# Copies of k issued by GpSimd, and each bias fetched behind the put of the squares, in the attention of a hybrid decoder block

## The chip, the cores and the metric

The kernel runs on one core of one Trainium2 chip. Times are device microseconds for one execution. The engines are TensorE (PE; its weight loads are PEld), VectorE (DVE), ScalarE (ACT), GpSimd (POOL) and SyncE (SP). SP does no arithmetic here: it issues most of the DMAs, strictly in order.

## The reference, cut to what matters

One layer of a decoder block on 512 tokens of width 1024: a retention branch and a forgetting-attention branch, merged by gates, then a feed-forward part. The change lies in the forgetting attention, which has 8 heads of width 64:

```python
c = jnp.cumsum(log_f, axis=1).transpose(0, 2, 1)
...
s = jnp.einsum('bhqd,bhkd->bhqk', q_blk, kh).astype(jnp.float32) * scale
s = s + c_blk[..., None] - c[:, :, None, :]
s = jnp.where(mask[None, None], s, -jnp.inf)
p = jax.nn.softmax(s, axis=-1)
return jnp.einsum('bhqk,bhkd->bhqd', p.astype(vh.dtype), vh)
```

All is float32. Queries come in 4 blocks of 128, and a block needs the keys up to its own end only.

## The kernel before, in words

**Products in three parts.** PE takes each float32 operand as a sum of a rounded high part and the rest, and forms high x high, low x high and high x low. Splitting a weight tile takes a cast on ACT (`wh<-raw`, L164) and a subtraction on DVE (`wl<-raw,wh`, L165). Two raw buffers and three pairs of split buffers go round. For the scores the split of q fills both halves of the partitions (high in one, low in the other), so one matmul does two of the three products if the high part of k stands in both halves as well. That is the copy of k: `fox_prep` casts k into one half of `tk` on ACT (L775) and a DMA copies this half into the other (L777). The low part of k goes into `kl`, whose other half GpSimd has set to zero (L991).

**The chain of a head.** The heads go in pairs `a` with `e` = 0, 1; here they are called heads 0 to 7. `chain` lists 32 steps, each head's query blocks from the last (512 keys) down to the first (128 keys). A step is: GpSimd adds the causal mask to 128 columns of the bias `cb` (L798); PE forms the scores into a bank `sc` or `tp`; DVE adds the bias, negates and finds the extremum (L804, tiles `pr` and `nm`); ACT takes the exponential (L806). Two steps later DVE transposes the weights in 32 x 32 squares into `psq` (L818). When a head's squares are all there, `fox_put` writes them to DRAM (`pd<-psq`) and `fox_get` reads them back with rows and columns exchanged in four DMAs (`pT<-pd`). For an odd head the reciprocal row sums go the same way (`rd<-rt`, `rw<-rd`, two DMAs). Then `fox_values` multiplies by v for a pair on PE, DVE scales (L857), ACT casts `ofh` and DVE subtracts `ofl` (L866).

**The bias.** `fox_bias(h)` reads one row of 512 numbers from DRAM (`cd`) into all 128 partitions of a `cb` buffer. There are three such buffers, so a bias waits for the one three heads before to be used up.

**What sets the order.** The instructions of PE are chained by hand (`in_order`), and between the steps of the attention `Fill` puts in matmuls of the gate projections, by a running account of time. SP's DMAs of this stage are chained in the order of the program (`move`, L71). The order on DVE, ACT and GpSimd, and the place of a bias among SP's DMAs, come from a scheduler that goes by the order of the program and by its own estimates.

**Completion counters.** DMAs of SP and ACT are counted on eight counters, DMAHW0 to DMAHW7, given out in turn. A DMA whose counter is still in use by an older one waits for that.

Of the kernel before, what the change touches and what calls it, by code (L numbers as in the profile page):

```python
# [23 lines left out]
FH, FD = 8, 64  # L24
# [27 lines left out]
def block_kernel(ctx: ExitStack, tc, x, xT, c_early, c_tab, c_late, w_vf, w_tok, w_vg, w_qk, w_a, w_y, w_o, w_gu, w_gl, w_dn, w_dh, out):  # L52
    nc = tc.nc
# [15 lines left out]
    def move(to, src):  # L69

        ins = nc.sync.dma_start(out=to, in_=src)  # L71
        if moves[0]:
            if moves[1] is not None:
                after(ins, moves[1])
            moves[1] = ins
        return ins
# [9 lines left out]
    def f32(ap):  # L86
        return ap.bitcast(F32)
# [72 lines left out]
    def split_raw(raw, width=1024):  # L160
        pool, bufs = next_pool(part_pools, 1)
        h = pool.tile([P, WP if pool is wp else 1024], F32R, name="wh", tag="wh", bufs=bufs)
        l = pool.tile([P, WP if pool is wp else 1024], F32R, name="wl", tag="wl", bufs=bufs)
        split_raw.last = (nc.scalar.copy(out=h[:, :width], in_=raw[:, :width]),  # L164
                          tt(out=l[:, :width], in0=raw[:, :width], in1=f32(h)[:, :width], op=ALU.subtract))  # L165
        return h, l
# [55 lines left out]
    for k in range(NK):  # L222
        h, l = first_units[k // 2]
# [274 lines left out]
    gp = nc.gpsimd  # L498
    ret = [{} for _ in range(NT)]
    fox = {}  # L500
# [215 lines left out]
    def fox_bias(h):  # L716

        cb = fwk.tile([P, S], F32, name="cb", tag="cb", bufs=CBUF)
        move(cb, cd[h:h + 1, :].broadcast_to([P, S]))
        return cb  # L720
# [42 lines left out]

    turn_next.n = 0

    def fox_prep(a, e, part):

        r, o = ((ra, rb), (rb, ra))[e]
        zr = (kf, qf)[part].rearrange("p c (u j) -> p u c j", j=32)[r, 4 * a:4 * a + 4]
        h = fwk.tile([P, S], F32R, name=("tk", "tq")[part], tag=f"{('tk', 'tq')[part]}{e}", bufs=2)  # L770

        def parted(f):
            return f.rearrange("p (u c j) -> p u c j", c=4, j=32)

        nc.scalar.copy(out=parted(h[r]), in_=zr)  # L775
        if part == 0:
            nc.scalar.dma_start(out=f32(h)[o], in_=f32(h)[r])  # L777
        to = h[o] if part else kls[a % 2][e][r]
        tt(out=parted(to), in0=zr, in1=parted(f32(h)[r]), op=ALU.subtract)
        fox[("k", "q")[part], a, e] = h  # L780
# [6 lines left out]
    def fox_scores(a, e, i):  # L787

        tq, tk, kl = fox["q", a, e], fox["k", a, e], kls[a % 2][e]
        if i == NT - 1:  # L790
            fox["cb"] = fox["bias"].pop(0)
            if e == 0:
                fox["rs", a] = sm.tile([P, 2, NT], F32, name="rs", tag="rs", bufs=2)
        cb = fox["cb"]
        n = (i + 1) * P
        m = max(n, 256)
        qs = slice(i * P, n)
        gp.tensor_tensor(out=cb[:, qs], in0=cb[:, qs], in1=mask, op=ALU.add)  # L798
        sc = next_bank()
        mm(sc[:, :m], lhsT=tq[:, qs], rhs=tk[:, :m], start=True, stop=False)  # L800
        mm(sc[:, :m], lhsT=tq[:, qs], rhs=kl[:, :m], start=False, stop=True)
        pr = fwk.tile([P, n], F32, name="pr", tag=f"pr{i}", bufs=1)
        nm = sm.tile([P, 1], F32, name="nm", tag="nm", bufs=4)
        fox_scores.last = nc.vector.tensor_tensor_reduce(out=pr[:, :n], in0=cb[:, :n], in1=sc[:, :n], scale=-1.0, scalar=3e38,  # L804
                                       op0=ALU.add, op1=ALU.min, accum_out=nm)
        fox["last"] = act(out=pr[:, :n], in_=pr[:, :n], func=AF.Exp, scale=-1.0, bias=nm, accum_out=fox["rs", a][:, e, i:i + 1])  # L806
        fox["pr", a, e, i] = pr

    def fox_turn(a, e, i):

        if i == NT - 1:
            fox["sq", a, e] = fwk.tile([P, 4, 10, 32], F32, name="psq", tag="psq", bufs=PSQ)
        pr, to = fox["pr", a, e, i], fox["sq", a, e].rearrange("p b c j -> p c b j")
        squares_ = pr.rearrange("p (k b j) -> p k b j", b=4, j=32)
        for k0, k1, step in ((0, min(i, 1), 3), (2, i, 1)):
            if k1 >= k0:
                c = TRI[k0] + i
                nc.vector.transpose(out=to[:, c:c + (k1 - k0) * step + 1:step], in_=squares_[:, k0:k1 + 1])  # L818

    def fox_put(a, e):  # L820

        pd = fox["pd", e] = drp.tile([4, 32, 4, 320], F32, name="pd", tag=f"pd{e}")
        move(pd.rearrange("g m b x -> (g m) (b x)"), fox["sq", a, e].rearrange("p b c j -> p (b c j)"))
        if e:
            nc.vector.reciprocal(out=ri[:, 0:2 * NT], in_=fox["rs", a].rearrange("p e i -> p (e i)"))
            rt = sm.tile([P, 32], F32, name="rt", tag="rt", bufs=1)
            nc.vector.transpose(out=rt, in_=ri)
            fox["rt"] = rt

    def put_scale():  # L830

        rd = fox["rd"] = drp.tile([P, 32], F32, name="rd", tag="rd")
        move(rd, fox["rt"])

    def fox_get(a, e):

        pT = fox["pT", a, e] = fwk.tile([P, 4, 320], F32, name="pT", tag="pT", bufs=PT)
        for b in range(4):
            move(pT[32 * b:32 * b + 32], fox["pd", e][:, :, b, :].rearrange("g m x -> m g x"))
        if e:  # L840
            rw = fox["rw", a] = fwk.tile([P, S], F32, name="rw", tag="rw", bufs=1)
            for h, rows in enumerate((ra, rb)):
                row = fox["rd"].rearrange("(g x) j -> x g j", g=4)[4 * h:4 * h + 4].rearrange("i g j -> g i j")
                row = bass.AP(tensor=row.tensor, offset=row.offset, ap=[[0, FD], [32 * 32, 4], [1, 4 * 32]])
                move(rw[rows].rearrange("p (g x) -> p g x", g=4), row)

    def fox_values(a):

        av = next_bank()
        o = av.rearrange("p (g i j) -> p g i j", g=4, i=NT)  # L850
        for k in range(NT):
            c = TRI[k] + k
            for e in range(2):
                mm(o[e * FD:(e + 1) * FD, :, k:, :].rearrange("p g i j -> p g (i j)"), lhsT=vf[:, k, (2 * a + e) * FD:(2 * a + e + 1) * FD],
                   rhs=fox["pT", a, e][:, :, 32 * c:32 * (c + NT - k)], start=k == 0, stop=k == NT - 1)
        o = o.rearrange("p g i j -> p i g j")
        first = tt(out=o, in0=o, in1=fox["rw", a].rearrange("p (g i j) -> p i g j", i=NT, g=4), op=ALU.mult)  # L857
        after(first, split_raw.last[1])
        if a == 3:
            after(first, y_ret.last)  # L860
        h, l = (f[:, a, :].rearrange("p (i g j) -> p i g j", i=NT, g=4) for f in (ofh, ofl))
        cast = nc.scalar.copy(out=h, in_=o)
        after(cast, split_raw.last[0])
        if a == 3:
            after(cast, sigmoid.last)
        tt(out=l, in0=o, in1=f32(h), op=ALU.subtract)  # L866
# [129 lines left out]
    fox["bias"] = [fox_bias(0)]  # L996
    for part in range(2):
        fox_prep(0, 0, part)
    fill(CF[3])
    fox["bias"].append(fox_bias(1))  # L1000
    fill(PF)
    chain = [(a, e, i) for a in range(4) for e in range(2) for i in reversed(range(NT))]
    for s in range(len(chain) + 10):
        a, n = s // 8, s % 8
        if n % 4 < 2 and s < 4:
            fox_prep(0, 1, n)
        if n % 4 in (2, 3) and a < 3:
            fox_prep(a + 1, n // 4, n % 4 - 2)
        if s < len(chain):
            fox_scores(*chain[s])  # L1010
            if n in (1, 5) and 2 * a + n // 4 + 2 < FH:
                fox["bias"].append(fox_bias(2 * a + n // 4 + 2))
        if n == 1 and a > 1:
            fill(VF)
            if a == 2:
                fill.until(8)
            if a == 5:
                ready.append(split_raw(begun.pop(0)))
            fox_values(a - 2)
        if n == 7 and a < 4 or n == 3 and 0 < a < 5:  # L1020
            fox_put(*chain[s - 7 + 3][:2])
        if n == 5 and 0 < a < 5:
            put_scale()
        if n in (2, 6) and 0 < a < 5:
            fox_get(*chain[s - 10 + 3][:2])
        if LAG <= s < len(chain) + LAG:
            fox_turn(*chain[s - LAG])
        fill(SF[chain[s][2]] if s < len(chain) else TAIL)
# [397 lines left out]
    for k in range(HALF + 2, NF):  # L1426
        n = k - HALF - 2
# [54 lines left out]
    for g in range(4):  # L1482
        if g < 3:
            ws.append(factors(w_dh[g + 1]))
        o = pf[:, g % 2, HALF + 4 * (g // 2):HALF + 4 * (g // 2) + 4, :]
# [142 lines left out]
```

## Time and profile before

| | us |
|---|---|
| median of 3 runs | 687.45 (686.4 to 688.64) |
| the profiled execution | 688.16 |
| its span, first to last instruction | 686.1 |
| stage of the change, from the first copy of k to the last scores | about 182 to 258 |

The granted clock of TensorE is 1.000. In the rows of the timelines the columns are the start in us, the duration in us, the engine (SPq and ACTq are the DMA queues of SP and ACT), the line, the operation, the tile written and the tiles read, how many instructions the row merges, and in brackets the idle time before and what ended it. In the chain of waits they are start, duration, and what. A row of waits gives the total in us, how many, and the longest.

### The profile page before, as it was taken

Reading aid. Unit: us, or ns where it says so; the run is one execution under the profiler, and the core shown is the slowest. Engines: PE = TensorE matmul, PEld = TensorE weight load, DVE = VectorE, ACT = ScalarE, POOL = GpSimd, SP = SyncE. Lnnn points to the kernel's source line nnn. Section 1 sums busy time; section 2 is a strip of 40 time slices with the busy share of each in tenths; the row PEclk is TensorE's granted clock in tenths of the full one; section 3 lists DMA queues with packets and bytes.
Section 4 is the critical chain, followed back from the end, with each engine's and each line's share of the span. In section 5 each row is a group of like instructions: output and inputs, shape, how many; then the busy total and the mean of one; then the engine's idle time right before and its main releaser. Section 6 shows DMA issues by size and latency. Waiting matters only on the chain.

```text
span 686.1 us, 9408 instructions
## 1 busy us (share of the span) xinstructions
PE 672.4 (98%) x3367; PEld 558.8 (81%) x3367; DVE 555.7 (81%) x882; ACT 372.9 (54%) x575; POOL 58.7 (9%) x73
## 2 busy tenths in 40 slices
PE   8999899999999899999999999999999999999998
PEld 5887688988886667788888888888888898888997
DVE  6899989986588675387989998989999888656794
ACT  6787655463665444454666655564647474443341
POOL 0033420000222110000130000000000000000000
PEclk9999999999999999999999999999999999999999
DMA  8906000651547787517710615546362523654221
GB/s 290 404 22 245 1 0 33 191 179 63 198 155 207 218 256 220 193 62 254 298 62 4 242 31 146 153 124 172 88 179 61 126 91 65 157 144 157 89 97 61
DMA packets 82926, 98.42 MB, mean 143 GB/s; under 512 B 52640, under 2 KB 60096, under 8 KB 82112
## 3 DMA queue, kind: packets, MB, share of 16 engines
q1 hardware_dynamic: 82096, 96.76, 44.1%
q10 hardware_dynamic: 784, 1.07, 0.5%
q8 instruction: 26, 0.43, 0.3%
q14 instruction: 20, 0.16, 0.1%
HBM read 81.45 MB, written 9.54 MB: 133 GB/s over the span
## 4 chain that ended last, share of the span: by engine, by line
PE 60%; DMA 4%; DVE 2%; ACT 1%; issue 1%; SPq 1%; DVEq 0%; ACTq 0%
PE acc L81 46%; PE sc L81 11%; PE tp L81 3%; DMA pd<-psq 2%; DMA raw<-in_w_a_dram 1%; DVE ps L1130 1%; DMA tk<-tk 1%; ACT ps L1129 1%; SPq L71 1%; DMA b<-in_w_gl_dram 0%; DVE b L1138 0%; DVE us L1332 0%; DVE us L1327 0%; DVE ofl L866 0%; ACT wh L164 0%
## 5 line engine op out<-in xcount | busy, mean ns | idle before, releaser
L81 PE MATMUL acc<-ps,xfh 128*128 128x512 f32 (+1 forms) x576 | 166.6, 372 | 0.3 <-ACT us L1251 0.3
L81 PEld LDWEIGHTS acc<-ps,xfh 128*128 128x128 f32 x576 | 105.2, 188 | 19.2 <-ACT us L1251 0.5
L1129 ACT CAST ps<-b 128x1024 fp32r<-128x1024 f32 (+1 forms) x84 | 82.3, 981 | 58.0 <-DVE b L1138 26.7
L1130 DVE TENSOR_TENSOR ps<-b,ps 128x1024 fp32r<-128x1024 f32 (+1 forms) x84 | 94.3, 1135 | 18.9 <-ACT ps L1129 17.8
L81 PE MATMUL acc<-ps,xfl 128*128 128x512 f32 (+1 forms) x288 | 106.9, 371 | 0.0
L164 ACT CAST wh<-raw 128x1024 fp32r<-128x1024 f32 (+1 forms) x36 | 37.7, 1049 | 46.0 <-DMA raw<-in_w_y_dram 13.5
L81 PEld LDWEIGHTS acc<-ps,xfl 128*128 128x128 f32 x288 | 54.3, 188 | 9.4
L165 DVE TENSOR_TENSOR wl<-raw,wh 128x1024 fp32r<-128x1024 f32 (+1 forms) x36 | 44.2, 1230 | 15.0 <-ACT wh L164 14.8
L1138 DVE TENSOR_TENSOR b<-b,b 128x1024 f32<-128x1024 f32 (+1 forms) x48 | 52.1, 1124 | 0.0
L81 PE MATMUL acc<-xh,wh 128*128 128x512 f32 x128 | 51.0, 399 | 0.0
L81 PE MATMUL acc<-xh,wl 128*128 128x512 f32 x128 | 50.1, 391 | 0.3 <-DVE wl L165 0.3
L81 PE MATMUL acc<-xl,wh 128*128 128x512 f32 x128 | 50.0, 391 | 0.0
L165 DVE TENSOR_TENSOR wl<-blk,wh 128x1024 fp32r<-128x1024 f32 x28 | 36.8, 1324 | 4.5 <-ACT wh L164 4.3
L81 PE MATMUL acc<-hl,ps 128*128 128x512 f32 x168 | 40.4, 389 | 0.0
L164 ACT CAST wh<-blk 128x1024 fp32r<-128x1024 f32 x28 | 29.3, 1049 | 14.3 <-DVE blk L372 5.3
L81 PEld LDWEIGHTS acc<-hl,ps 128*128 128x128 f32 x168 | 31.5, 188 | 6.6
L81 PE MATMUL acc<-wl,xh 128*128 128x512 f32 (+2 forms) x104 | 33.8, 326 | 1.4 <-DVE wl L165 1.4
L1251 ACT COPY us<-acc 128x512 f32<-128x512 f32 (+1 forms) x48 | 26.1, 550 | 16.3 <-PE acc L81 15.3
L81 PE MATMUL acc<-wh,xh 128*128 128x512 f32 (+2 forms) x104 | 34.4, 331 | 0.0
L81 PE MATMUL acc<-wh,xl 128*128 128x512 f32 (+2 forms) x104 | 33.7, 324 | 0.0
L1177 DVE TENSOR_TENSOR ps<-raw,ps 128x1024 fp32r<-128x1024 f32 x14 | 17.1, 1219 | 18.8 <-ACT ps L1174 18.8
L81 PEld LDWEIGHTS acc<-xh,wl 128*128 128x128 f32 x128 | 24.0, 188 | 6.0 <-DVE wl L165 0.7
(304 smaller groups left out, 1514.0 us busy)
## 6 DMA issues: line engine op xcount, KB each, us to landing
b<-in_w_gu_dram SPq DMA_DIRECT2D x40, 512.0 KB, 4.5
raw<-in_w_a_dram SPq DMA_DIRECT2D x16, 512.0 KB, 4.6
raw<-in_w_dn_dram SPq DMA_DIRECT2D x14, 512.0 KB, 3.8
pd<-psq SPq DMA_DIRECT2D x8, 640.0 KB, 6.6
pT<-pd SPq DMA_DIRECT2D x32, 160.0 KB, 3.3
pf<-squares SPq DMA_DIRECT2D x160, 32.0 KB, 1.9
blk<-in_w_vg_dram SPq DMA_DIRECT2D x8, 512.0 KB, 10.3
blk<-in_w_qk_dram SPq DMA_DIRECT2D x8, 512.0 KB, 4.2
```

Of the source, the lines that this page charges most:

```text
L71: ins = nc.sync.dma_start(out=to, in_=src)
L81: in_order(nc.tensor.matmul(o, **kw))
L164: split_raw.last = (nc.scalar.copy(out=h[:, :width], in_=raw[:, :width]), tt(out=l[:, :width], in0=raw[:, :width], in1=f32(h)[:, :width], ...
L165: tt(out=l[:, :width], in0=raw[:, :width], in1=f32(h)[:, :width], op=ALU.subtract))
L1129: part.cast = nc.scalar.copy(out=h, in_=raw)
L1130: low = tt(out=l, in0=raw, in1=f32(h), op=ALU.subtract)
L1138: queue(tt(out=raws[g][b][v], in0=raws[g][b][v], in1=raws[g][c][v], op=ALU.add))
L1177: tt(out=l, in0=raw, in1=f32(h), op=ALU.subtract)
L1251: copy = nc.scalar.copy(out=u_(tp, slot), in_=os[tp][:, :w])
```

## The change

The copy of k isn't issued by ACT behind its cast any more. `fox_prep` only notes it down, and `flush` issues what is noted from GpSimd: once ahead of the chain, and then in each step behind the step's scores, and so behind its mask add. The bias of head h + 2 was asked for in the second step of head h; now it is asked for in the last step, behind the put that this step may contain. All else is the same: what is computed, the number of DMAs and their sizes.

```diff
+    later = []
+
+    def flush():
+        while later:
+            h, o, r = later.pop(0)
+            gp.dma_start(out=f32(h)[o], in_=f32(h)[r])
+
     def fox_prep(a, e, part):
 ...
         nc.scalar.copy(out=parted(h[r]), in_=zr)
         if part == 0:
-            nc.scalar.dma_start(out=f32(h)[o], in_=f32(h)[r])
+            later.append((h, o, r))
 ...
     for part in range(2):
         fox_prep(0, 0, part)
+    flush()
     fill(CF[3])
 ...
         if s < len(chain):
             fox_scores(*chain[s])
-            if n in (1, 5) and 2 * a + n // 4 + 2 < FH:
-                fox["bias"].append(fox_bias(2 * a + n // 4 + 2))
+            flush()
 ...
         if n == 7 and a < 4 or n == 3 and 0 < a < 5:
             fox_put(*chain[s - 7 + 3][:2])
+        if n % 4 == 3 and 2 * a + n // 4 + 2 < FH:
+            fox["bias"].append(fox_bias(2 * a + n // 4 + 2))
         if n == 5 and 0 < a < 5:
             put_scale()
```

How the order moves, first on SP, from the put of head 0 to the put of head 2. Tiles carry a number here; in brackets stand the engines and counters that the instruction waits for. Before:

```order
L71 DMA cb_2026<-cd_1758 128x512 [waits DMAHW7_49,DMAHW1_49,DVE_49]
L71 DMA pd_2068<-psq_1979 128x1280 [waits DMAHW3_49,DVE_49]
L71 DMA cb_2103<-cd_1758 128x512 [waits DMAHW4_49,DVE_49]
L71 DMA raw_2111<-in_w_a_dram 128x1024 [waits DMAHW6_49,Activation_49]
...
L71 DMA pd_2150<-psq_2047 128x1280 [waits DMAHW4_49,DVE_49]
L71 DMA cb_2187<-cd_1758 128x512 [waits DMAHW6_49,DVE_49]
...
L71 DMA rw_2215<-rd_2189 64x4x128 [waits DMAHW7_49]
L71 DMA rw_2215<-rd_2189 64x4x128 [waits DMAHW5_49]
L71 DMA pd_2235<-psq_2133 128x1280 [waits DMAHW6_49,DVE_49]
```

Now:

```order
L71 DMA pd_2066<-psq_1977 128x1280 [waits DVE_49]
L71 DMA cb_2068<-cd_1758 128x512 [waits DMAHW7_49,Pool_49]
L71 DMA raw_2109<-in_w_a_dram 128x1024 [waits DMAHW2_49,Activation_49]
...
L71 DMA pd_2148<-psq_2045 128x1280 [waits DMAHW4_49,DVE_49]
L71 DMA cb_2153<-cd_1758 128x512 [waits Pool_49]
...
L71 DMA rw_2213<-rd_2187 64x4x128 [waits DMAHW6_49,DMAHW3_49]
L71 DMA rw_2213<-rd_2187 64x4x128
L71 DMA pd_2233<-psq_2131 128x1280 [waits DMAHW5_49,DVE_49]
```

The bias of head 3 (`cb_2026`, now `cb_2068`) stood ahead of the put of head 0 and stands behind it; that of head 4 (`cb_2103`, now `cb_2153`) has moved from ahead of head 1's put to behind it. The second `rw` waited for counter 5 and waits for none.

On GpSimd, from the last memset of `kl` on, before (`cb_1848`, `cb_1879`, `cb_1952`, `cb_2026`, `cb_2103` are the biases of heads 0 to 4):

```order
L991 MEMSET kl_1821 64x512
L798 TENSOR_TENSOR cb_1848<-cb_1848,ctab_95 128x128
L798 TENSOR_TENSOR cb_1879<-cb_1879,ctab_95 128x128
L798 TENSOR_TENSOR cb_1952<-cb_1952,ctab_95 128x128
L798 TENSOR_TENSOR cb_1848<-cb_1848,ctab_95 128x128 x3
L798 TENSOR_TENSOR cb_1879<-cb_1879,ctab_95 128x128
L798 TENSOR_TENSOR cb_2026<-cb_2026,ctab_95 128x128
L798 TENSOR_TENSOR cb_1879<-cb_1879,ctab_95 128x128 x2
L798 TENSOR_TENSOR cb_1952<-cb_1952,ctab_95 128x128
L798 TENSOR_TENSOR cb_2103<-cb_2103,ctab_95 128x128
L798 TENSOR_TENSOR cb_1952<-cb_1952,ctab_95 128x128 x2
```

Now (heads 0 to 3 are `cb_1848`, `cb_1879`, `cb_1994`, `cb_2068`):

```order
L998 MEMSET kl_1821 64x512
L771 DMA tk_1850<-tk_1850 64x512
L805 TENSOR_TENSOR cb_1848<-cb_1848,ctab_95 128x128
L805 TENSOR_TENSOR cb_1879<-cb_1879,ctab_95 128x128
L771 DMA tk_1920<-tk_1920 64x512
L771 DMA tk_1965<-tk_1965 64x512
L771 DMA tk_2033<-tk_2033 64x512
L805 TENSOR_TENSOR cb_1994<-cb_1994,ctab_95 128x128
L805 TENSOR_TENSOR cb_1848<-cb_1848,ctab_95 128x128 x3
L771 DMA tk_2114<-tk_2114 64x512
L805 TENSOR_TENSOR cb_1879<-cb_1879,ctab_95 128x128 x3
L771 DMA tk_2196<-tk_2196 64x512
```

Four copies go out ahead of the third head's first add; the others stand between the adds. The first add of head 3 stood inside head 1's adds and now comes behind them, ahead of head 2's second (its row follows the last one shown).

## The prediction, made before the result was known

> **What bounds the kernel now.** I began with the page: is TensorE (PE) the bound?
>
> ```profile
> PE 672.4 (98%) x3367; PEld 558.8 (81%) x3367; DVE 555.7 (81%) x882; ACT 372.9 (54%) x575; POOL 58.7 (9%) x73
> ```
>
> PE is busy 98% of a span of 686.1 us. A change elsewhere can gain only where PE stands still. Both edits act in the forgetting attention, so I read PE's own timeline there, 178 to 262 us, for starts that are too far apart.
>
> ```profile
> 215.84 0.39 PE L81 MATMUL acc<-xh,wl 128*128 128x512 f32 x1
> 216.49 0.45 PE L81 MATMUL sc<-tk,tq 128*128 128x384 f32 x1 [0.27 <-DVE nm L804]
> ...
> 220.49 1.07 PE L81 MATMUL tp<-pT,vf 128*64 128x512 f32 x2
> 223.10 2.34 PE L81 MATMUL tp<-pT,vf 128*64 128x512 f32 x14 [1.55 <-DMA pT<-pd]
> ...
> 230.13 0.39 PE L81 MATMUL acc<-xl,wh 128*128 128x512 f32 x1
> 230.35 0.39 PE L81 MATMUL acc<-xh,wl 128*128 128x512 f32 x1
> 231.23 0.41 PE L81 MATMUL tp<-tk,tq 128*128 128x384 f32 x1 [0.49 <-DVE ofl L866]
> ...
> 232.58 0.40 PE L81 MATMUL acc<-xl,wh 128*128 128x512 f32 x1
> 233.28 0.50 PE L81 MATMUL acc<-xh,wl 128*128 128x512 f32 x1 [0.29 <-DVE wl L165]
> ...
> 237.06 0.39 PE L81 MATMUL acc<-xh,wl 128*128 128x512 f32 x1
> 238.47 0.44 PE L81 MATMUL tp<-tk,tq 128*128 128x384 f32 x1 [1.02 <-DVE nm L804]
> ...
> 241.75 1.07 PE L81 MATMUL sc<-pT,vf 128*64 128x512 f32 x2
> 244.12 2.34 PE L81 MATMUL sc<-pT,vf 128*64 128x512 f32 x14 [1.30 <-DMA pT<-pd]
> ```
>
> Neighbours in full flow start about 0.23 us apart (230.13 to 230.35). Taking 0.23 off each gap (0.46 where the row holds two matmuls), the stalls are 0.42, 2.15, 0.65, 0.47, 1.18 and 1.91: **6.8 us** in all, which is the most that any repair here can give. The two long ones wait for pT, the transposed weights of the softmax on their way back from DRAM. What delays those? The chain of waits goes back to one copy of k:
>
> ```profile
> 220.25 3.93 DMA tk<-tk
> ...
> 224.20 0.59 SPq L71
> ...
> 224.89 4.43 DMA pd<-psq
> ...
> 231.18 8.15 DMA pd<-psq
> ```
>
> The copy was issued by ACT at 220.25 and landed at 224.18; SyncE (SP), which has nothing to do with k, went on at 224.20 and only then put head 2's squares (224.89). SP's own waits, in 219 to 225 us and then in 209 to 211 us, name the two tiles of this change:
>
> ```profile
> SPq L71 <- DMA tk<-tk: 4.3, 2, 3.9
> ```
> ```profile
> SPq L71 <- DMA cb<-cd: 2.0, 1, 2.0
> ```
>
> The reason stands in the order of the instructions: DMAs of SP and ACT are counted on eight completion counters in turn, and a DMA whose counter is still in use waits for that older one. Before, the second rw waits for the counter that a copy of k holds, and the put of head 1 waits for the counter of the bias issued before it. As SP works in order, all that follows waits too.
>
> ```profile
> 201.54 0.33 SPq L71 DMA_DIRECT2D pd<-psq  x1
> ...
> 210.48 0.34 SPq L71 DMA_DIRECT2D pd<-psq  x1
> ...
> 217.52 2.05 SPq L71 DMA_DIRECT2D pT<-pd  x4
> 219.61 5.18 SPq L71 DMA_DIRECT2D rw<-rd  x2
> ...
> 231.18 0.47 SPq L71 DMA_DIRECT2D pd<-psq  x1
> ...
> 239.41 1.74 SPq L71 DMA_DIRECT2D pT<-pd  x4
> 241.25 1.24 SPq L71 DMA_DIRECT2D rw<-rd  x2
> ```
>
> Each pT starts when its put has landed (210.48 to 217.52; 231.18 to 239.41), so a put that leaves sooner brings its PE wait forward.
>
> **The change part by part.**
>
> *Copies off the shared counters.* The eight copies now count on counters of GpSimd's own. In the new order the second rw waits for no counter. The later pair of rw took 1.24 us, the blocked one 5.18: SP is through **3.9 us** sooner, and the put of head 2 with it.
>
> *Bias behind the put.* The put of head 1 loses its wait for a bias (it still names counter 4, but eight DMAs back on it stands a weight load from long before). What else holds it is head 1's last transpose on DVE:
>
> ```profile
> 209.24 0.63 DVE L818 STREAM_TRANSPOSE psq<-pr 128x128 f32<-128x128 f32 x2
> ```
>
> The first of these two ends about 209.5, so the put leaves near 209.6 and not 210.48: **0.9 us**, and the first pT wait on PE ends that much sooner. DVE's chain may shrink too, as GpSimd (POOL) no longer takes head 4's first mask add ahead of head 2's third; I count nothing for it.
>
> *Carried on.* Put of head 2: 0.9 + 3.9 = 4.8 us sooner. Put of head 3: SP could issue it 4.8 sooner, at 226.4, but head 3's last transpose holds it:
>
> ```profile
> 226.64 0.30 DVE L818 STREAM_TRANSPOSE psq<-pr 128x128 f32<-128x128 f32 x1
> ```
>
> That ends at 226.94, so 231.18 becomes 226.9, **4.3 us** sooner, and pT lets PE go on at 244.12 - 4.3 = 239.8. PE itself gets there at 241.75 + 0.46 = 242.2, less 0.9 (first pT) and less 0.65 + 0.47 + 1.18, whose causes (rw, weights and transposes queued behind the put of head 2) all move about 4 us: 239.0. So it still waits 0.8, and has gained 4.3. From 252 us on the chain of waits has rows of PE alone, up to this one, so the gain stays:
>
> ```profile
> 512.46 24.49 PE acc L81 x108
> ```
>
> *What the copies cost on POOL.* No row before shows a DMA issued by POOL. Bounds: from below the issue on ACT, 0.47 us; from above the landing of a copy, 3.5 us at the least, as if POOL were held until then.
>
> ```profile
> L777 ACTq DMA_DIRECT2D tk<-tk x8: 468/468/535, 182.6 to 220.3; - x8
> ...
> DMA to landing us min/median/max: 3.5/4.2/7.3
> ```
> ```profile
> L798 POOL TENSOR_TENSOR cb<-cb,ctab x32: 453/462/1445, 186.1 to 257.3; 128x128 f32<-128x128 f32 x32
> ...
> DMA to landing us min/median/max: 3.5/5.2/6.9
> ```
> ```profile
> 182.06 2.25 POOL L991 MEMSET kl<- 64x512 f32 x4 [69.71 <-DVE orl L340]
> ...
> 201.04 0.46 POOL L798 TENSOR_TENSOR cb<-cb,ctab 128x128 f32<-128x128 f32 x1 [1.81 <-DVE nm L804]
> ...
> 207.73 0.46 POOL L798 TENSOR_TENSOR cb<-cb,ctab 128x128 f32<-128x128 f32 x1 [2.48 <-DVE nm L804]
> ...
> 214.14 0.46 POOL L798 TENSOR_TENSOR cb<-cb,ctab 128x128 f32<-128x128 f32 x1 [1.71 <-DVE nm L804]
> ```
>
> I take 1 us, nearest to the two rows for one instruction (0.47 on ACT, 0.45 to 1.45 on POOL). Four copies go out before the scores begin; four stand between mask adds, ahead of which POOL sat idle for about 1.7 to 1.8 us (201.04 and 214.14 are two of these places). At 1 us they fit: cost **0**. Without that cover it would be up to 4 x 1 us on DVE's chain. The first copy has to wait for the memsets, to 184.31 instead of 182.60, and PE wants it here:
>
> ```profile
> 191.93 0.39 PE L81 MATMUL tp<-tk,tq 128*128 128x512 f32 x1
> ```
>
> That leaves 7.6 us against a landing of 3.5 to 7.3: hidden. ACT loses eight issues of 0.47, which lie beside other work: 0.
>
> *Bias later.* A bias is issued right behind the put before it and lands 5.2 us later. Head 3's: 201.54 + 0.5 + 5.2 = 207.2, and its add now stands just ahead of head 2's second add, which ran at 207.73: it fits with 0.5 us to spare. The other heads' adds come later against their puts: 0.
>
> **Sum**: 4.3 us off the profiled execution, which took 688.16 (span 686.1), gives 683.9; the median of the runs shown, 687.45, lies 0.7 lower: 683.2.
>
> [...]
>
> **Rivals.**
>
> *1. Another wait takes the place of the lane.* SP gets past rw, but the put of head 2, or pT behind it, is then held by DVE or by slower landing (a put took 4.43 in one case and 8.15 in another, so 3.7 us of the 4.3 can be lost to crowded queues). Then what stays is 0.9 at most: 687.45 - 0.9 = **686.5**. For it: each stall on PE has DVE or a DMA close behind. Against it: head 2's last transposes were long done, and nothing but pT and rw stood ahead of its put:
>
> ```profile
> 214.43 0.69 DVE L818 STREAM_TRANSPOSE psq<-pr 128x256 f32<-128x256 f32 x2 [0.37 <-ACT pr L806]
> ```
>
> *2. Slower: POOL is held by its copies.* Place: the mask adds queued behind four copies, for which DVE waits, and for DVE the scores on PE. For it: the add took 0.45 at best and 1.45 at worst, so something on this engine can triple. Price: at 3.5 us a copy, each costs 3.5 - 1.8 = 1.7 us, four 6.8, against the gain of 4.3: +2.5, **690.0**. It decides from 1.8 + 4.3 / 4 = 2.9 us a copy. Against it: the copy is a single plain instruction, and ACT issued it in 0.47.
>
> [...]
>
> *3. The bias comes too late.* At a landing of 6.9 instead of 5.2, head 3's add is 1.2 us late and holds head 2's second add; once more for a later head, and 2.4 of the gain of 4.3 is gone: 687.45 - 1.9 = **685.5**. For it: the margin of 0.5. Against it: the bias no longer crowds the transfer of the put that follows.
>
> *That the change doesn't do what it says*: none of this holds if SP's second rw still waits for a copy; the new order rules that out.
>
> **How the numbers follow.** Forecast **683.2 us**, chance 0.55; its own range is 680.7 (all 6.8 us of stalls gone) to 685.3. Rival 1: 0.18, rival 2: 0.16, rival 3: 0.11. A measurement can tell 0.3% (2.1 us, so 685.4 and 689.5) from no change. Faster: 0.53 of the forecast, 0.05 of rival 3, whose time lies on that edge, and 0.03 of rival 1: 0.61. Slower: 0.15 of rival 2, whose 690.0 lies past the other edge, and 0.01 of rival 1: 0.16. Within: what is left, 0.23. The range for 8 in 10 runs from 680.7, the bound of the stalls, to 688.6, which takes in rivals 1 and 3 with some spread and leaves rival 2 out.
>
> **What would show it.** Right: no wait of SP for tk; rw pair near 1.2 us; put of head 2 before 221 and of head 3 before 228; PE's two pT stalls 2.15 and 1.91 down to about 1.7 and 0.8, and those at 231, 233 and 238 gone. Wrong: a POOL copy over 1.8 us with DVE waiting for cb behind it; PE waiting for a copy ahead of the first scores; a put of head 2 that still leaves after 223.

## The result

The changed kernel took **681.99 us** (median of five runs, 680.9 to 683.58) against 687.45 (five runs, 686.4 to 688.64) before: ratio **0.9916**, 95% interval 0.9899 to 0.9934. The ratios compare the runs of a series and need not equal the quotient of the two medians. Two later series with the same kernel gave 0.9930 (0.9914 to 0.9946) and 0.9925 (0.9902 to 0.9947). The profiled execution took 683.1 us with a span of 681.0, 5.1 less than before. From the page of the changed kernel, the busy time of the engines:

```profile
PE 671.0 (99%) x3367; PEld 558.7 (82%) x3367; DVE 555.5 (82%) x882; ACT 372.4 (55%) x575; POOL 65.5 (10%) x81
```

PE's own timeline in the attention (start, duration, instruction, idle time before it):

```profile
220.34 2.37 PE L81 MATMUL tp<-pT,vf 128*64 128x512 f32 x16
222.65 0.50 PE L81 MATMUL acc<-xh,wh 128*128 128x512 f32 x1
...
228.62 0.40 PE L81 MATMUL acc<-xh,wl 128*128 128x512 f32 x1
229.35 0.50 PE L81 MATMUL acc<-xh,wh 128*128 128x512 f32 x1 [0.34 <-ACT wh L164]
229.68 0.40 PE L81 MATMUL acc<-xl,wh 128*128 128x512 f32 x1
230.61 0.50 PE L81 MATMUL acc<-xh,wl 128*128 128x512 f32 x1 [0.53 <-DVE wl L165]
...
237.80 1.07 PE L81 MATMUL sc<-pT,vf 128*64 128x512 f32 x2
239.09 1.37 PE L81 MATMUL sc<-pT,vf 128*64 128x512 f32 x6 [0.22 <-DMA pT<-pd]
```

The first wait for pT (2.15 us behind 220.49 before) is gone: all 16 matmuls run in one piece. By the same reckoning as in the prediction, 0.50, 0.70 and 0.83 us are left of the stalls, 2.0 instead of 6.8. SP's timeline tells why (each row is one issue or a group of them):

```profile
201.97 0.88 SPq L71 DMA_DIRECT2D raw<-in_w_a_dram  x1
204.56 1.75 SPq L71 DMA_DIRECT2D pT<-pd  x4
209.79 0.34 SPq L71 DMA_DIRECT2D pd<-psq  x1
...
213.19 2.52 SPq L71 DMA_DIRECT2D pT<-pd  x4
216.16 1.36 SPq L71 DMA_DIRECT2D rw<-rd  x2
217.62 0.55 SPq L71 DMA_DIRECT2D pd<-psq  x1
...
218.74 1.72 SPq L71 DMA_DIRECT2D raw<-in_w_a_dram  x2
...
225.90 0.43 SPq L71 DMA_DIRECT2D pd<-psq  x1
...
234.47 1.74 SPq L71 DMA_DIRECT2D pT<-pd  x4
```

The pair of rw takes 1.36 us (5.18 before), so the put of head 2 leaves at 217.62 (224.89). The put of head 1 left only 0.69 us sooner (209.79 against 210.48), but it landed in 3.4 us instead of 7.0, and its pT could start at 213.19 (217.52). The second is a step that the prediction did not have.

Not everything behind the put of head 2 came that much sooner. The first of the two weight loads there left at 218.74, 6.7 us sooner than before:

```profile
225.48 0.43 SPq L71 DMA_DIRECT2D raw<-in_w_a_dram  x1
```

But it took 9.5 us to land instead of 5.4, and the cast on ACT, which waits for it, began only 2.7 us sooner (230.91 before):

```profile
228.25 1.05 ACT L164 CAST wh<-raw 128x1024 fp32r<-128x1024 f32 x1 [2.25 <-DMA raw<-in_w_a_dram]
```

PE was 3.5 us ahead of before by then (228.62 against 232.12 for the same matmul). The stalls of 0.50 and 0.70 us are its waits for the high and then the low part of this weight.

On GpSimd the eight copies look like this (duration min/median/max in ns, then the landing), with DVE's waits for a mask add in 185 to 262 us and two of the adds behind the bias of head 3:

```profile
L771 POOL DMA_DIRECT2D tk<-tk x8: 516/532/736, 184.7 to 218.1; - x8
...
DMA to landing us min/median/max: 2.2/5.4/8.3
```
```profile
DVE pr L811 <- POOL cb L805: 4.4, 13, 0.6
```
```profile
206.32 0.80 POOL L805 TENSOR_TENSOR cb<-cb,ctab 128x128 f32<-128x128 f32 x1 [0.39 <-DMA cb<-cd]
207.61 0.46 POOL L805 TENSOR_TENSOR cb<-cb,ctab 128x128 f32<-128x128 f32 x1 [0.49 <-DVE nm L811]
```

A copy holds GpSimd for 0.53 us, about as long as it held ACT (0.47 to 0.54). No wait of DVE for a mask add exceeds 0.6 us; before, they were 6.4 us in all and up to 1.6.

### The profile page after: what moved, and what is told of

It is laid out like the page before. It is cut to its first block, busy times and chain, and to the rows that moved or that the text cites. A ratio compares the mean times of both kernels' runs of the same rounds, so it can differ in the third digit from the quotient of the medians.

```text
span 681.0 us, 9438 instructions
## 1 busy us (share of the span) xinstructions
PE 671.0 (99%) x3367; PEld 558.7 (82%) x3367; DVE 555.5 (82%) x882; ACT 372.4 (55%) x575; POOL 65.5 (10%) x81
## 4 chain that ended last, share of the span: by engine, by line
PE 84%; DVE 5%; DMA 4%; ACT 3%; issue 2%; POOL 1%; SPq 0%; DVEq 0%; ACTq 0%; POOLq 0%
PE acc L81 65%; PE sc L81 14%; PE tp L81 5%; DMA pd<-psq 2%; DMA raw<-in_w_tok_dram 1%; DVE wl L165 1%; POOL cb L805 1%; DVE pr L811 1%; DVE ps L1139 1%; ACT wh L164 1%; ACT ps L1138 1%; PE tp L84 1%; DMA pT<-pd 0%; DMA b<-in_w_gl_dram 0%; DVE psq L825 0%
## 5 line engine op out<-in xcount | busy, mean ns | idle before, releaser
L813 ACT ACTIVATE pr<-pr,nm 128x512 f32<-128x512 f32 (+3 forms) x32 | 18.0, 562 | 21.2 <-DVE nm L811 21.1
```

## What made the put of head 1 land sooner

The share of the DMA engines in 205 to 217 us, in 40 slices of 0.3 us (each digit in tenths), before and after:

```profile
DMA  0000025325764798999999999999999999878499
```
```profile
DMA  9997789999999896003998999394999799856799
```

Before, the engines are full from about 209.5 to 215, across the put at 210.48. After, the DMA engines stand still from 209.8 to 210.4, just when the put leaves. The traffic ahead of the put is the bias of head 4 (256 KB), a weight load (512 KB) and the four pT of head 0 (160 KB each). Before, these came together on SP at 205.61, 206.02 and 206.49, after a pause of SP from the put of head 0 (201.54) on. After, what is left of them comes at 201.97 and 204.56. What SP paused for, the experiments had to show.

The landings tell how the traffic acts. In the traces of the two kernels all 116 DMAs that SP issued from 182 to 262 us (58 each) land in the order in which they left, so a put lands behind the last transfer ahead of it. The six puts of heads 1 to 3 in these traces go by how long that transfer still had to go when the put left. With 1.0 us to go the put took 3.4 us, with 2.9 us (in both kernels) 4.4 and 4.9, with 5.7 us 7.0, and with 7.0 and 7.1 us 8.15 and 8.5. Ahead of the put of head 1 the last pT of head 0 had 5.7 us to go before (it landed at 216.17) and 1.0 after (210.75).

## The experiments

Ratios are to the kernel before on the same chip, in the same series; its medians in the three series of experiments are 689.18, 687.7 and 688.16 us, so times of different series are not compared as they stand. The changed kernel stands beside them with 0.9916, 0.9930 and 0.9925.

**Each part alone.** First the copies on GpSimd, with the biases where they were:

```diff
+            if n in (1, 5) and 2 * a + n // 4 + 2 < FH:
+                fox["bias"].append(fox_bias(2 * a + n // 4 + 2))
...
-        if n % 4 == 3 and 2 * a + n // 4 + 2 < FH:
-            fox["bias"].append(fox_bias(2 * a + n // 4 + 2))
```

> Only the copies of k go to GpSimd; the biases are asked for where they were before, so the weight load stands behind the bias of head 4 again and leaves 4 us later than in the changed kernel. Theory A (copies free SP's second rw; the bias order is what uncrowds the put of head 1): rw pair near 1.3 us and the put of head 2 near 219 us, but the put of head 1 takes over 6 us to land again and PE's first pT stall of about 2 us stays: 684.0 us. Theory B (the copies alone give everything): first pT stall gone too, 682.0 us.

Measured: 685.57 us, ratio 0.9941 (0.9923 to 0.9959). SP's timeline:

```profile
209.23 0.34 SPq L71 DMA_DIRECT2D pd<-psq  x1
...
216.48 2.63 SPq L71 DMA_DIRECT2D pT<-pd  x4
219.20 1.36 SPq L71 DMA_DIRECT2D rw<-rd  x2
```

The wait at rw is gone, the put of head 1 still lands in 7.2 us. Then the biases behind the puts, with the copies on ACT:

```diff
-            later.append((h, o, r))
+            nc.scalar.dma_start(out=f32(h)[o], in_=f32(h)[r])
```

> Only the biases move behind the puts; the copies of k are issued by ACT as before. Theory A: the weight load leaves near 202 us, the put of head 1 lands in under 4 us, the first pT stall (2.15 us) is gone; and as the moved biases also shift which counter falls to which DMA, the second rw no longer meets the copy: between 682.5 and 685.0 us. Theory B (the copies on the shared counters are all that matters, wherever the bias stands): SP still waits for tk, 687 us. The prediction's own price for this part was 0.9 us: 686.5 us.

Measured: 684.41 us, ratio 0.9926 (0.9910 to 0.9942). SP's timeline, and its waits in 198 to 228 us (in total, times, longest):

```profile
208.66 0.34 SPq L71 DMA_DIRECT2D pd<-psq  x1
...
212.84 2.54 SPq L71 DMA_DIRECT2D pT<-pd  x4
...
217.60 0.60 SPq L71 DMA_DIRECT2D pd<-psq  x1
220.91 0.34 SPq L71 DMA_DIRECT2D cb<-cd  x1
```
```profile
SPq L71 <- DMA tk<-tk: 4.2, 3, 2.7
```

The put of head 1 lands in 4.2 us. SP still waits for copies of k, 4.2 us in all, but the longest of these waits now stands at the bias behind the put of head 2, which nobody needs soon. With the biases in other places another DMA comes to the turn of the copy's counter, and the pair of rw takes 2.13 us instead of 5.18. So the parts overlap: each alone gives most of the gain (0.6% and 0.7%), and both together 0.7 to 0.8%. Moving the biases removes the harm of the shared counter too, by a shift in the turn.

**One bias alone.** Head 4's bias is the one that stands between the puts of heads 0 and 1 before. In the changed kernel this one alone was put back to its old place, and in the kernel before this one alone was moved:

```diff
 changed kernel:
+            if s == 9:
+                fox["bias"].append(fox_bias(4))
...
-        if n % 4 == 3 and 2 * a + n // 4 + 2 < FH:
+        if n % 4 == 3 and 2 * a + n // 4 + 2 < FH and s != 11:
 kernel before:
-            if n in (1, 5) and 2 * a + n // 4 + 2 < FH:
+            if n in (1, 5) and 2 * a + n // 4 + 2 < FH and s != 9:
...
+        if s == 11:
+            fox["bias"].append(fox_bias(4))
```

> The changed kernel, with the bias of head 4 alone put back to its old place (behind the second score of head 2, two scores ahead of the put of head 1). There SP waits for the buffer of that bias until DVE has read head 1's last scores. Theory, that this wait is what made the put of head 1 slow before (the weight load and the four pT of head 0 queue behind it on SP and are still in flight when the put leaves): SP waits about 3.5 us ahead of the bias, the weight load leaves near 205.5 and not 202, the pT of head 0 near 206, the put of head 1 lands in 6 to 7.5 us and not 3.4, the first wait of PE for pT comes back with 0.5 to 2 us; ratio 0.9935 to 0.996. Rival, that the put lands sooner because no bias of its own size leaves close behind or ahead of it, or for another reason that one bias doesn't carry: landing stays under 4.5 us, ratio as the changed kernel's.

> The kernel before, with the bias of head 4 alone moved behind the put of head 1; all other biases and the copies as before. Theory of the wait for the bias buffer: the weight load leaves near 202, the put of head 1 lands in under 5 us, the first wait of PE for pT (2.15 us) is gone. In the new order neither the two rw nor the put of head 2 shares a counter with a copy of k, so the later waits shrink too: ratio 0.991 to 0.9945, as with all biases moved. Rival, that only moving all the biases does it: landing near 7 us, ratio 0.996 to 1.000.

Put back: 686.28 us, ratio 0.9968 (0.9952 to 0.9985). Moved alone: 683.15 us, ratio 0.9925 (0.9907 to 0.9943), as much as the whole change. SP's timeline and its waits in 198 to 228 us, with the bias put back:

```profile
201.81 4.37 SPq L71 DMA_DIRECT2D cb<-cd  x2
206.27 0.38 SPq L71 DMA_DIRECT2D raw<-in_w_a_dram  x1
206.71 2.21 SPq L71 DMA_DIRECT2D pT<-pd  x4
210.27 0.34 SPq L71 DMA_DIRECT2D pd<-psq  x1
...
217.22 1.81 SPq L71 DMA_DIRECT2D pT<-pd  x4
```
```profile
SPq L71 <- DVE nm L811: 3.6, 1, 3.6
```

And with it moved alone:

```profile
201.59 0.51 SPq L71 DMA_DIRECT2D raw<-in_w_a_dram  x1
...
209.20 0.34 SPq L71 DMA_DIRECT2D pd<-psq  x1
...
212.80 4.47 SPq L71 DMA_DIRECT2D pT<-pd  x4
```

That settles the pause. The biases have three buffers (CBUF = 3), so head 4's needs the buffer of head 1, and SP waits at its DMA until DVE has read head 1's last scores (3.6 us; in the kernel before the profile puts 4.0 us at this place down to DVE). The weight load and the pT of head 0 wait behind it and are still under way when the put of head 1 leaves: it lands in 6.9 us with the bias put back, in 3.5 with it moved. Where the bias stands behind the put, its buffer is free by then: in the changed kernel SP waits for DVE's `nm` no more than 0.2 us in 198 to 228 us.

Two things came out otherwise than expected. With the bias put back the kernel lost 3.4 us against the changed one (686.28 against 682.92). PE's first wait for pT came back with 0.8 us only; larger are 1.8 and 0.7 us at the weight split, where the load behind the put of head 2 landed 9.7 us after its issue. The profiled execution also lost 1.7 us by the clock (last section), but the clock doesn't explain the series: six of the twelve runs have a mean clock of 1.000, and their median, 685.9, is still 3.0 us behind. With the bias moved alone SP still waits for copies of k, 5.0 us in two waits, one of 2.9 among the pT of head 1 (in the 4.47 above) and one of 2.1 at the weight load. As expected, neither rw nor the put of head 2 waits for a copy there, but these two do.

**Is it crowding alone?** One transfer of 512 KB more, right ahead of the put of head 1, in the changed kernel:

```diff
+        if (a, e) == (0, 1):
+            move(drp.tile([P, 1024], F32, name="crowd"), w_a[0, 0, 0])
```

> The changed kernel, with one transfer more: 512 KB from the weights to a scratch area in DRAM, issued by SP right ahead of the put of head 1. Nobody reads it. Theory, that the put of head 1 lands in 3.4 us (and not 7.0) because no weight load crowds it: with the extra transfer the put lands in 6 to 9 us, the first wait of PE for pT comes back with 1.5 to 3.5 us, and 1 to 3 us of the gain go: ratio 0.994 to 0.996. Rival, that the put lands sooner because it leaves sooner, whatever else is in flight: landing stays under 4.5 us, no wait for pT at that place, ratio 0.990 to 0.993 with the issue of one DMA (0.4 us) on SP as the only cost.

Measured: 683.1 us, ratio 0.9932 (0.9919 to 0.9944), no slower than the changed kernel. The extra transfer was still under way (206.22, landing in 6.0 us) when the put left:

```profile
206.22 0.64 SPq L71 DMA_DIRECT2D crowd<-in_w_a_dram  x1
209.67 0.35 SPq L71 DMA_DIRECT2D pd<-psq  x1
...
213.92 1.75 SPq L71 DMA_DIRECT2D pT<-pd  x4
```

The put took 4.2 us instead of 3.4: 0.8 for these 512 KB, not 3.6. So the bytes ahead of the put don't explain the 7.0 by their number alone. It is the time that they still have to go: the extra transfer had 2.6 us left when the put went out, and the pT of head 0 had landed or nearly so (4.6 to 5.4 us after issues at 204.4 to 205.7). Before, the pT had 3.7 to 5.7 us to go (7.7 to 8.3 us after issues at 206.5 to 207.9, behind the weight load, which landed at 212.77). Nor does leaving sooner do it alone, as the rival had it: with head 4's bias put back the put left at 210.27, 0.2 us sooner than before, and took 6.9. Why the four pT take as long as they do was not tried.

**Does the wait belong to the counter, or to rw?** In the kernel before, one tiny DMA between the two rw:

```diff
             for h, rows in enumerate((ra, rb)):
+                if a == 0 and h:
+                    move(drp.tile([1, 32], F32, name="shift"), fox["rd"][0:1])
```

> The kernel before, with one tiny DMA (128 bytes, DRAM to DRAM, used by nobody) that SP issues between the two rw of head 1. Copies and biases as before. It takes the second rw's place in the turn of the eight counters, so in the new order it is the tiny one that waits for the counter of the copy of k; the second rw then has a counter of another DMA. Theory of the shared counter: SP now waits about 3.9 us at the tiny DMA, the put of head 2 leaves no sooner than 224.5, the same time as before: ratio 0.998 to 1.002. Rival, that the wait of 3.9 us belongs to the second rw's own data (the row sums written just ahead): the tiny DMA goes out at once and the second rw still takes 5 us; the time is the same too, so the rows tell it, not the time.

Measured: 688.69 us, ratio 1.0013 (1.0004 to 1.0022). SP's timeline and its waits in 198 to 228 us:

```profile
219.24 0.71 SPq L71 DMA_DIRECT2D rw<-rd  x1
223.88 0.55 SPq L71 DMA_DIRECT2D shift<-rd  x1
224.48 0.63 SPq L71 DMA_DIRECT2D rw<-rd  x1
```
```profile
SPq L71 <- DMA tk<-tk: 4.3, 2, 3.9
```

The same 3.9 us now stand at the tiny DMA, which shares nothing with k but the counter, and the second rw goes out right behind it. The wait belongs to the place in the turn, as the prediction read it.

**What holding GpSimd costs.** First a second copy behind each, into scratch DRAM; then extra adds of 128x128 behind each of the last four copies, six and twelve, on a tile that nobody needs:

```diff
             gp.dma_start(out=f32(h)[o], in_=f32(h)[r])
+            for _ in range(1):
+                extra[0] += 1
+                gp.dma_start(out=drp.tile([FD, S], F32, name=f"extra{extra[0]}"), in_=f32(h)[r])
 in the other two, behind each of the last four copies (12 in the second; also a memset of the tile and one small DMA at the end):
+                for _ in range(6):
+                    after(gp.tensor_tensor(out=hold, in0=hold, in1=mask, op=ALU.add), one)
```

> The changed kernel with a second copy of the same half of k behind each copy, into scratch DRAM that nobody reads, so twice the issue time on GpSimd and 1 MB more traffic. Theory (an issue on GpSimd holds it for about 0.53 us and lies in its idle time): 682.0 us, within 0.7 us of the changed kernel. Rival (each issue is on DVE's path): four more issues of 0.53 between the mask adds, 2.1 us slower, 684.1 us.

> The changed kernel with six more adds of 128x128 (0.46 us each, on a spare tile) behind each of the last four copies, so that GpSimd is held about 0.53 + 2.8 = 3.3 us a copy; one small DMA to scratch at the end. By the price of the prediction's second rival, 4 x (3.3 - 1.8) = 6.0 us slower than the changed kernel: 688.0 us, with DVE waiting for cb at these places. Other theory (PE runs four score steps ahead of DVE and DVE has waits of its own, so most is absorbed): not over 2 us slower, 682 to 684 us.

> The changed kernel, with twelve extra adds of 128x128 on GpSimd behind each of the last four copies (six in the earlier run), on a tile that nobody needs: GpSimd is held about 6.1 us a copy instead of 0.53. Where six adds cost 1.7 us against the changed kernel. Theory, that PE's lead over the mask adds (about four scores) takes up the first 3 us of each hold and the rest comes through in full: four times 2.8 us more, less what stalls already there take up: 8 to 13 us over the changed kernel, ratio 1.003 to 1.012. Rival, that what comes through stays a small share (about 0.15 of the hold, as with six adds): 3 to 4 us over the changed kernel, ratio 0.996 to 0.998. The prediction's own formula, 4 x (t - 1.8): 17 us, ratio 1.017.

Measured: 684.24 us, ratio 0.9931 (0.9914 to 0.9948) with a second copy; 685.1 us, 0.9942 (0.9928 to 0.9956) with six adds; 696.07 us, 1.0124 (1.0110 to 1.0139) with twelve. GpSimd's groups in 190 to 245 us (number, busy time in us, mean in ns, idle time before), and DVE's waits for it in 185 to 262 us, with six adds and then with twelve:

```profile
L775 POOL TENSOR_TENSOR pad<-pad,ctab 128x128 f32<-128x128 f32 x24 | 12.8, 534 | 1.3
L771 POOL DMA_DIRECT2D tk<-tk x4 | 2.1, 534 | 1.7 <-ACT tk L786 1.6
```
```profile
DVE pr L815 <- POOL cb L809: 8.9, 16, 2.2
```
```profile
L775 POOL TENSOR_TENSOR pad<-pad,ctab 128x128 f32<-128x128 f32 x48 | 24.6, 513 | 3.1
```
```profile
DVE pr L815 <- POOL cb L809: 19.2, 16, 4.2
```

The second copy can't be told from none: its ratio lies within the intervals of the changed kernel, and the rival's 684.1 us would be 0.9951 of 687.45, outside its own. (The 684.24 us as such is no hit for the rival, as the kernel before took 689.18 in that series; the changed kernel was not timed in it.)

The copies themselves take 2.1 us with six adds and with twelve. With its adds a copy holds GpSimd (12.8 + 2.1) / 4 = 3.7 us, or (24.6 + 2.1) / 4 = 6.7. The first costs 0.8 to 1.8 us over the changed kernel (0.9942 less 0.9930, 0.9925 or 0.9916, of 687.45), which the intervals hardly tell from nothing; the second costs 13.0 (696.07 less 683.06 in the same series). So nearly 4 us a copy are taken up, and beyond that most comes through: some 11 us for 4 x 3.0, about 2 of them by the clock (last section). A straight line between 1.8 and 13.0 puts the point where the gain of 5 us is used up at about 4.6 us a copy; that is an estimate, and the adds stood in two or three pieces between the mask adds, not in one block as one long copy would.

**The changed kernel again**, for its level beside the others:

> The changed kernel word for word, beside the next three, for their level. Both theories: ratio to before 0.990 to 0.994, as when it was first timed (0.9916).

> The changed kernel word for word, for the level beside the two runs with the bias of head 4. Both theories: ratio 0.990 to 0.994 (0.9916 and 0.9930 so far).

Measured: 683.06 us (681.19 to 685.08) and 682.92 us (680.84 to 684.44), the ratios given at the top. No kernel tried here is measurably faster than the changed one.

## Why the prediction was right, and where its steps were not

- **The time.** 683.2 forecast, 681.99 measured; the gain 4.3 against 5.1 in the profiled executions and 4.6 to 5.5 by the medians of the three series.
- **Copies off the shared counters.** Right, with its size: rw pair 1.36 us, 3.8 sooner through, and no wait for tk on SP. The tiny DMA showed that the wait was the counter's.
- **"The put of head 1 ... 0.9 us, and the first pT wait on PE ends that much sooner."** This step failed. The put left 0.7 sooner, as its transposes allowed, but landed 3.6 us sooner. The step looked only at what the put itself waits for and kept its landing constant. It missed that moving head 4's bias takes a wait of 3.6 us for a buffer from ahead of the weight load and the pT of head 0, behind which the put then had to land. The row that pointed there was in the trace: SP did nothing from the put of head 0 (201.54) to 205.61. The first pT stall, foreseen at 1.7, is zero, and the put of head 2 left 7.3 us sooner instead of 4.8.
- **The sum of the stalls** was taken too small, and with it the 6.8 us as "the most that any repair here can give". The prediction took 0.46 us off a gap with two matmuls. In the trace the 16 matmuls on pT start in pairs, 0.01 us apart, when all pT are there, and take 2.31 us in all (220.34 to 222.65); before, they took 4.88 (220.49 to 225.37) and 4.64 (241.75 to 246.39). So the two waits cost 2.6 and 2.3 us, not 2.15 and 1.91, and the 0.83 that is left costs 1.3. Counted so, the stalls fell from 7.6 to 2.5 us, close to the 5.1 by which the span is shorter.
- **Carried on.** The put of head 3, foreseen at 226.9, left at 225.90 and landed in 8.5 us (8.15 before). PE still waits 0.83 at its pT, where 0.8 was foreseen. That these agree is luck: PE came there 4.0 us sooner and not 3.2, and in the profiled execution of the third series the 16 matmuls run in one piece there too, with no wait.
- **The stalls between.** Of 0.65 + 0.47 + 1.18 us, foreseen as gone, 0.65 and 1.18 went. The 0.47 at the weight split became 0.50 + 0.70. The prediction was right that the weight load moves with the put of head 2 (it left 6.7 us sooner), and again kept its landing constant: 9.5 us instead of 5.4. One thing goes with the longer landing: with the later bias order head 5's bias leaves right ahead of this load on SP (218.21), while before it left ahead of the put of head 2 (212.83). In the later order the load took 9.5 us in the changed kernel, 9.7 with head 4's bias put back and 6.2 with the biases alone moved; in the old order it took 5.4 in the kernel before and 5.6 with the copies alone. That this is the cause was not tried by itself.
- **Copies on POOL.** Taken at 1 us, measured 0.53 (0.74 at most), and hidden; a second copy behind each was hidden as well, as far as the ratio can tell.
- **Bias of head 3.** Its first add waited 0.39 us for the bias, and head 2's second add came at 207.61 (207.73 before). The margin held.
- **Rival 1** (another wait takes over; 686.5) did not come about; slower landing did show, but at the weight load (9.5 us instead of 5.4). The copies alone gave 0.6% (0.9941). Where the biases had moved already, the same edit gave nothing that can be measured (0.9926 against 0.9916 to 0.9930); there the longest wait for a copy, 2.7 us, stood at a bias that nobody needed soon.
- **Rival 2** (POOL held; 690.0 at 3.5 us a copy) was priced too dear. At 3.7 us a copy the kernel is still at 0.9942: the formula 4 x (t - 1.8) gives 7.6 us there and at most 1.8 were measured; at 6.7 it gives 19.6 and 13.0 were measured. It charged each copy's overhang in full to PE. That PE has other matmuls to run meanwhile may be why less comes through; this was not tried by itself.
- **Rival 3** (bias too late) did not come about, by the margin above.

So that the number came out near is in part luck, since two errors partly offset: the first wait for pT gave 2.6 us where 0.9 was foreseen, and the weight split cost 0.7 us more than before where 0.5 less was foreseen. The split of the gain over the two parts was wrong. The prediction had the copies bring a put forward by 3.9 us and the bias by 0.9; measured alone, the copies give 0.6% (4 us) and head 4's bias alone 0.75% (5 us), and they overlap.

## What to carry to other kernels

On a DMA queue that issues in order, as SP's does here, list for every DMA all that it waits for, its buffer included, and then what stands behind it: here a bias asked for before its buffer was free held all that stood behind it on SP for 3.6 us. A DMA that leaves at another time also stands behind other traffic (the put of head 1 left 0.7 us sooner and landed in 3.4 us instead of 7.0; the weight load left 6.7 us sooner and took 9.5 instead of 5.4), so don't carry its old landing time over; look at what is still ahead of it on its queue when it leaves, and how long that has to go. When completion counters are handed out in turn, as here, a DMA added or moved can change who waits for whom (one tiny DMA took over the wait of 3.9 us from rw), and a gain measured for one edit can be had by another (the copies alone 0.9941, the biases alone 0.9926).

## What was not expected of the hardware

PE's granted clock was 1.00 all through this stage in the profiled executions of the kernel before and of the changed one, but not in all experiments. From the run with head 4's bias put back, in stretches of 2 us (bounds, length, busy time and count of PE, PEld, DVE, ACT and POOL, then the clock, the DMA share and GB/s):

```profile
230.00:232.00 2.00, 0.86 (x4) 0.38 (x3) 0.90 (x4) 0.57 (x1) 0.58 (x2) 1.00 1.03 222
232.00:234.00 2.00, 0.95 (x3) 0.52 (x4) 1.50 (x2) 2.00 (x8) 0.00 (x0) 1.00 0.99 350
234.00:236.00 2.00, 2.00 (x9) 1.67 (x9) 1.72 (x5) 1.61 (x4) 0.46 (x1) 0.63 0.35 124
236.00:238.00 2.00, 2.00 (x6) 1.58 (x6) 0.90 (x5) 1.04 (x4) 0.75 (x2) 0.52 0.06 23
```

PE was busy for 1.81 of the 4 us from 230 to 234, with two stalls of 1.8 and 0.7 us, and then the clock was 0.63 and 0.52 for 2 us each: 0.37 x 2 + 0.48 x 2 = 1.7 us lost on top of the stalls (an estimate from these rows), about half of what this execution is longer than that of the changed kernel (span 684.2 against 681.0). With twelve adds the clock was at 0.50 from about 237.3 to 244.1 us, after a stall of 2.81 us that ended at 236.15; PE had work from 239.9 on, with matmuls 0.43 us apart and not 0.23, so about 2 us were lost. The kernel before has a stall of 2.15 us with fuller work around it (PE busy for 2.45 of the 4 us from 220 to 224), and no such dip: 1.00 there and in the 4 us behind. In the run with the bias put back no single stall was longer than 1.8 us. There the two stalls and the low clock behind them together took more than the stalls' own length, which the prediction's sum of stalls had no term for. What brings the low clock, and how little work it takes, is not shown: these two traces have 1.81 of 4 us with it and 2.45 without.
